# Two extra matmuls of 320 contiguous columns in a decoder-layer kernel: one a weight tile behind the first norm's sums, one a weight tile behind the prompt's value products

## The chip, the cores and the metric

The kernel runs on one core of a Trainium2 chip. Time is device microseconds of one execution. The time before is the median of three runs; a profile is of one execution of its own.

## The reference

One decoder layer is computed for 256 prompt tokens and 8 x 8 sample tokens, 320 columns in all, that share the same weights (D = 2048, feed-forward width 5632, all float32):

- xn = RMSNorm(x), and one projection W_in gives B, C, h (1024 each), q (16 heads of 64), k and v (4 heads of 64), and two gates of 2048.
- Branch A: u = C * h, a causal convolution of width 3, times B, times W_conv_out.
- Branch B: attention in a window of 128 with a relative-position bias and a sink per head, times W_attn_out. The prompt attends in two blocks of 128 queries, the sample over cached keys and values.
- m = sigmoid(gate_conv) * A + sigmoid(gate_attn) * B, then x = x + W_o(m).
- x = x + SwiGLU(RMSNorm(x)), and a final RMSNorm.

Outputs are both groups' y and the new key, value and convolution states.

## The kernel before, in words

**Products.** Activations lie transposed: a tile of 128 features by 320 tokens. Each float32 operand is split into a high part (rounded by ScalarE, `whi`, `xh`) and the rest (VectorE subtracts, `wlo`, `xl`), and a product is three matmuls: high by high, low activations by high weights, high activations by low weights. `product` (L162) makes two output blocks of 128 features at a time. It goes over weight tiles of 4 x 128 rows by 256 columns, each loaded by a DMA (`wraw`), split by ScalarE (L129) and VectorE (L130), and used by 24 matmuls (L176). The matmuls take the activations in an order of 4 x 5 x 16 columns (`turns(fives(...))`), 320 in all. In the trace a product bears the name of its output tile: q, C, H, B, gc, ga, yc, ya, wo, fg, fu; kv is `kv_product` (L372).

**Order.** The program text is the order of the work. Products follow one another: kv, q (4 pairs of blocks), then four rounds of C, H and B, then eight of gc, ga, yc, ya, then wo, then the feed-forward part. The small work between them is written as generators. After each weight tile `product` calls `tick` (L145), which takes the next step of the generator that is current, and holds that step behind the tile's last matmul:

```
def tick():
    if side_work[0] is not None:
        with after(*last.values()):
            next(side_work[0], None)
```

A `yield` in a generator therefore means one weight tile later. During the q products the generator is `kv_work`, which begins with `first_norm`; during C, H and B it is `attention`: the prompt's scores (L549, L552, tiles ps), `prompt_values` with `prompt_pv` (L611, tiles po), then `sample_attention`: scores (L716, tiles pss) and values (L779, tiles spo).

**The first norm.** In its first step `first_norm` prepares the sums of squares; a step later two matmuls against ones (`over_partitions`, L199 and L200, tile prb) sum them over the partitions, and VectorE and ScalarE make the root. Then it yields three times.

**The value products.** `prompt_values` loads the turned probabilities, one unit at a step, then calls `prompt_pv`: 80 small matmuls into four PSUM tiles, po, which ScalarE and VectorE (L642, L643) then read out. It yields once and ends, and `sample_attention` starts in the same step that the end falls in.

**The nudge.** `nudge` (L193) is a matmul whose result nobody reads. It takes the first rows of one tile as 320 contiguous columns, against 128 columns of another, and writes a tile of the pool `aux`, which has four PSUM banks taken in turn by prb, ps, po, pss, spo and the nudges. Three are there before: in `kv_product` ahead of the sixth weight tile's work (L353), in `sample_attention` a step behind the scores (L727), and in it a step behind the values (L800).

Of the kernel before, what the change touches and what calls it, by code (L numbers as in the profile page):

```python
# [17 lines left out]
T = TP + NB * TS  # L18
# [34 lines left out]
def hybrid_layer(ctx: ExitStack, tc: tile.TileContext, a: dict, o: list):  # L53
# [18 lines left out]
    def ps_aux(name):  # L72
        return aux[0].tile([P, 512], F32, tag="aux", name=name)
# [3 lines left out]
    def u(s):  # L77
        uid[0] += 1
        return f"{s}_{uid[0]}"
# [36 lines left out]
    def row_tiles(pool, names, n, lead, tags=None):  # L116

        step = n * JS + 16
        size = -(-(lead + NS * step) // JS) * JS
        tiles = [pool.tile([P, size], F32R, tag=t, name=n_) for n_, t in zip(names, tags or names)]  # L120
        return [rows_in(t, lead, step, lambda k: k * JS) for t in tiles]
# [65 lines left out]
    def two_rows(src, hi, lo):  # L187

        nc.scalar.activation(hi, fives(src), AF.Copy)
        nc.vector.tensor_sub(fives(lo), fives(src), hi.bitcast(F32))  # L190
        return hi, lo

    def nudge(rows, weights, n):  # L193
        x, w = (bass.AP(r.tensor, r.offset, [list(r.ap[0]), [1, m]]) for r, m in ((rows(0), n), (weights(0), P)))
        nc.tensor.matmul(ps_aux(u("nudge"))[:, :n], w, x, start=True, stop=True)

    def over_partitions(out, parts):
        hi, lo = parts
        nc.tensor.matmul(turns(fives(out)), ones_r, turns(hi), start=True, stop=False)  # L199
        nc.tensor.matmul(out, ones_r, lo, start=False, stop=True)  # L200
# [22 lines left out]
    def rstd_of(ss, shape, name, pool, out=None):  # L223

        v = pool.tile(shape, F32, tag=f"rs_v{shape[1]}", name=u(name))
        nc.vector.tensor_scalar(v, ss, 1.0 / D, EPS, op0=ALU.mult, op1=ALU.add)
        return inv_root(v, shape, name, pool, out)
# [26 lines left out]
    xh, xl = row_tiles(xp, ("xh_t", "xl_t"), KC, LEAD_X, ("xh", "xl"))  # L254
# [139 lines left out]
    def squares(*chunks):  # L394

        for k in chunks:
            t = tmp("t" + "abcd"[k % 4], "sq")[:, :T] if k else xacc
            nc.scalar.activation(t, hT[:, k, :], AF.Square)
            if k:
                nc.vector.tensor_add(xacc, xacc, t)  # L400
# [32 lines left out]
    def first_norm():  # L433

        squares(12, 13, 14, 15)
        nc.vector.tensor_scalar(nsink, sink_bc, -1.0, None, op0=ALU.mult)
        e_sb = pr.tile([P, 2, 2 * WIN], F32, tag="w", name="e_sb", bufs=1).rearrange("p g k -> p (g k)")[:NH, :EL]
        nc.vector.memset(e_sb, NEG)
        parts = two_rows(xacc, at_h(7), at_t[:, LEAD_A + 6 * at_row:LEAD_A + 6 * at_row + T])
        at, one_each = [_bucket(c) for c in range(WIN)], NBK // 2  # L440
        nc.gpsimd.tensor_copy(e_sb[:, WIN - 1:WIN - 1 + one_each], relT[:, :one_each])
        for b in range(one_each, NBK):
            c, n = WIN - 1 + at.index(b), at.count(b)
            nc.gpsimd.tensor_copy(e_sb[:, c:c + n], relT[:, b:b + 1].to_broadcast([NH, n]))
        yield
        prb = ps_aux("prb")
        over_partitions(prb[:, :T], parts)
        rstd_of(prb[:, :T], [P, T], "r1", spare, out=rb)
        nc.vector.tensor_scalar(rbq, rb, HD ** -0.5, None, op0=ALU.mult)
        for z in (vT, kT):  # L450
            for c in range(2):
                nc.vector.tensor_mul(z[:, c, :], z[:, c, :], rb)
        nc.vector.tensor_mul(rbsq, rb, rb)
        nc.gpsimd.dma_start(e_scr, e_sb)
        nc.gpsimd.dma_start(
            bias_s, bass.AP(e_scr.tensor, e_scr.offset + WIN - TS, [[EL, NH], [1, TS], [1, WIN + TS]])
        )
        for _ in range(3):
            yield

    yp = ExitStack()
    yy = yp.enter_context(tc.tile_pool(name="yy", bufs=1))
# [135 lines left out]
    def prompt_masked(sides, pt, side):  # L598

        late = by_head(pt[:, :, 2:4])  # L600
        for out, m in ((side, 0), (late, 1)):
            mask = sides[:, m].rearrange("p (a j) -> p a j", j=B).unsqueeze(1).to_broadcast([P, 2, 4, B])
            nc.vector.tensor_mul(out, late, mask)

    def prompt_pv(pts, side, vm):
        po, step = [ps_aux(u("po")) for _ in range(4)], 2 * JS + 16

        def add(bank, kv, cols, w, x, start, stop):
            vals = slice(kv * HD, (kv + 1) * HD)
            out = po[bank][kv % 2 * 64:kv % 2 * 64 + 64, cols]  # L610
            nc.tensor.matmul(  # L611
                out.rearrange("p (g a j) -> p g a j", g=2, j=B), w[:, vals], x, start=start, stop=stop
            )

        for bank in range(4):
            for par in range(2):
                kv = bank // 2 * 2 + par
                add(bank, kv, slice(0, 256), vn[0], by_head(pts[kv][:, bank % 2, :, 0:2]), True, False)
        for whole in (True, False):
            for j in range(2):  # L620
                cols = slice(256 + j * 128, 384 + j * 128)
                for bank in range(4):
                    rows = slice(0, P) if whole else slice(bank * B, (bank + 1) * B)
                    for kv in (2 * j, 2 * j + 1):
                        x = pts[kv][:, :, bank, 2:4] if whole else side[kv][rows, :, :, bank]
                        add(bank, kv, cols, vm[bank] if whole else vn[0][rows], x, False, not whole and j == 1)
        for bank in range(4):
            src = po[bank][:, 0:256].rearrange("p (g s j) -> p g s j", g=2, j=JS)
            dst = at_chunks(2 * bank, 2)[:, :, 0:2 * step].rearrange("p g (s j) -> p g s j", s=2)
            two_to(dst[:, :, :, 0:JS], dst[:, :, :, JS:2 * JS], src)  # L630
        for bank in range(4):
            src = po[bank][:, 256:512].rearrange("p (c j) -> p c j", j=B)
            o = (2 + bank // 2) * step + bank % 2 * B
            two_to(*(at_chunks(0, 8)[:, :, o1:o1 + B] for o1 in (o, o + JS)), src)
# [27 lines left out]
    def prompt_values(pv, scrs):  # L662
        sides = pv.tile([P, 2, WIN], F32, name="sides")
        nc.gpsimd.memset(sides, 1.0)
        nc.gpsimd.affine_select(
            out=sides[:, 0], in_=sides[:, 0], compare_op=ALU.is_ge, fill=0.0, base=-1, pattern=[[-1, WIN]],
            channel_multiplier=1,
        )
        nc.gpsimd.affine_select(
            out=sides[:, 0], in_=sides[:, 0], compare_op=ALU.is_ge, fill=0.0, base=B - 1, pattern=[[B, 4], [0, B]],  # L670
            channel_multiplier=-1,
        )
        nc.gpsimd.tensor_tensor(sides[:, 1], sides[:, 1], sides[:, 0], op=ALU.subtract)
        pts = [pv.tile([P, 2, 4, 4, B], F32, name=f"pT{kv}") for kv in range(NKV)]
        side = [pv.tile([P, 2, 2, 4, B], F32, name=f"side{kv}") for kv in range(NKV)]
        vm = [pv.tile([P, DKV], F32, name=f"vm{t}") for t in range(3)] + [vn[1]]
        mixes = ((0, 0, P, 0), (0, 0, B, 1), (1, 0, P, 0), (1, 0, 2 * B, 1), (2, 0, P, 1), (2, 3 * B, P, 0))
        for i in range(len(units) + 5):
            if i < len(units):
                kv, gp = units[i]  # L680
                nc.gpsimd.dma_start(pts[kv][:, gp].rearrange("p a n j -> p (a n j)"), scrs[i])
            if 2 <= i < 8:
                t, r0, r1, src = mixes[i - 2]
                nc.scalar.activation(vm[t][r0:r1], vn[src][r0:r1], AF.Copy)
            if i >= 5:
                kv, gp = units[i - 5]
                prompt_masked(sides, pts[kv][:, gp], side[kv][:, gp])
            yield
        prompt_pv(pts, side, vm)
        yield  # L690

    W2 = WIN + TS

# [132 lines left out]
    def kv_work():  # L826
        yield from first_norm()
        rows = []
        for t in range(3):
            rows.append(kv_turn(t))  # L830
            yield
        yield from keys_twice()
        for t in range(3):
            kv_natural(t, rows[t])
            yield
# [190 lines left out]
    def h_parts(k):  # L1026
        return parts_of(hT[:, k, :])
# [250 lines left out]
    for c in (2, 3):  # L1278
        k = E0 // P + c
        first, _ = h_parts(k)  # L1280
# [53 lines left out]
def _bucket(dist):  # L1334
    half = NBK // 2
    if dist < half:
        return dist
    return min(half + int(math.log(dist / half) / math.log(WIN / half) * (NBK - half)), NBK - 1)
# [61 lines left out]
```

## Time and profile before

| | |
|---|---|
| median of 3 runs | 1590.14 us (1590.08 to 1590.64) |
| profiled execution | 1589.86 us |
| its span, first to last instruction | 1588.1 us |
| mean granted TensorE clock | 0.999 |
| TensorE busy | 1580.0 us, 99%, 11315 matmuls |
| VectorE, ScalarE, GpSimd busy | 881.6, 651.4, 128.5 us |
| read from HBM | 257.25 MB, 168 GB/s with the writes |

A matmul's duration in the trace (301 ns for 320 columns) is longer than its slot, because matmuls overlap. What counts is the distance from one start to the next. The chain of waits merges neighbouring matmuls of a line into one row with a length and a count, and length over count is that distance.

### The profile page before, as it was taken

Reading aid. Unit: us, or ns where it says so; the run is one execution under the profiler, and the core shown is the slowest. Engines: PE = TensorE matmul, PEld = TensorE weight load, DVE = VectorE, ACT = ScalarE, POOL = GpSimd, SP = SyncE. Lnnn points to the kernel's source line nnn. Section 1 sums busy time; section 2 is a strip of 40 time slices with the busy share of each in tenths; the row PEclk is TensorE's granted clock in tenths of the full one; section 3 lists DMA queues with packets and bytes.
Section 4 is the critical chain, followed back from the end, with each engine's and each line's share of the span. In section 5 each row is a group of like instructions: output and inputs, shape, how many; then the busy total and the mean of one; then the engine's idle time right before and its main releaser. Section 6 shows DMA issues by size and latency. Waiting matters only on the chain.

```text
span 1588.1 us, 27217 instructions
## 1 busy us (share of the span) xinstructions
PE 1580.0 (99%) x11315; PEld 1566.3 (99%) x11315; DVE 881.6 (56%) x1263; ACT 651.4 (41%) x913; POOL 128.5 (8%) x228
## 2 busy tenths in 40 slices
PE   9999999999999999999999999999999999999998
PEld 9999999999999999999999999999999999999887
DVE  7888765544455445565555555553443455555556
ACT  7554444333333334344333333333333333344443
POOL 2223242000000003320000000000000000000000
PEclk9999999999999999999999999999999999999999
DMA  8666666454444544444444445455555544544653
GB/s 276 204 191 193 213 205 207 160 157 157 152 158 159 159 158 153 156 158 160 157 153 156 158 159 159 154 154 158 159 159 156 155 157 158 160 159 152 186 191 122
DMA packets 77714, 266.09 MB, mean 168 GB/s; under 512 B 9816, under 2 KB 13240, under 8 KB 77464
## 3 DMA queue, kind: packets, MB, share of 16 engines
q1 hardware_dynamic: 71880, 249.86, 49.7%
q0 software_dynamic: 5280, 13.82, 2.9%
q8 instruction: 88, 1.44, 0.4%
q10 hardware_dynamic: 432, 0.69, 0.1%
q14 instruction: 34, 0.28, 0.1%
HBM read 257.25 MB, written 9.04 MB: 168 GB/s over the span
## 4 chain that ended last, share of the span: by engine, by line
PE 99%; DVE 0%; ACT 0%; DVEq 0%; issue 0%
PE fu L176 19%; PE fg L176 19%; PE dn L1059 12%; PE wo L176 7%; PE ga L176 7%; PE gc L176 7%; PE B L176 3%; PE H L176 3%; PE C L176 3%; PE q L176 3%; PE ya L176 3%; PE yc L176 3%; PE dn L1084 3%; PE kv L372 2%; PE dn L1092 2%; PE dl L1088 1%
## 5 line engine op out<-in xcount | busy, mean ns | idle before, releaser
L130 DVE TENSOR_TENSOR wlo<-wraw,whi 128x1024 fp32r<-128x1024 f32 (+1 forms) x460 | 560.9, 1220 | 574.3 <-ACT whi L129 563.4
L129 ACT ACTIVATE whi<-wraw 128x1024 fp32r<-128x1024 f32 (+1 forms) x460 | 485.0, 1056 | 699.5 <-PE fu L176 131.5
L176 PE MATMUL fu<-hh_t,whi 128*128 128x320 f32 x704 | 205.0, 301 | 0.0
L176 PE MATMUL fu<-hl_t,whi 128*128 128x320 f32 x704 | 205.0, 301 | 0.0
L176 PE MATMUL fg<-hh_t,whi 128*128 128x320 f32 x704 | 205.0, 301 | 0.0
L176 PE MATMUL fg<-hl_t,whi 128*128 128x320 f32 x704 | 205.0, 301 | 0.0
L1059 PE MATMUL dn<-a_t,whi 128*128 128x320 f32 x896 | 162.6, 301 | 0.0
L176 PE MATMUL fg<-hh_t,wlo 128*128 128x320 f32 x704 | 158.8, 301 | 0.0
L176 PE MATMUL fu<-hh_t,wlo 128*128 128x320 f32 x704 | 158.8, 301 | 0.0
L1059 PEld LDWEIGHTS dn<-a_t,whi 128*128 128x128 f32 x896 | 137.5, 187 | 0.0
L176 PEld LDWEIGHTS fu<-hh_t,whi 128*128 128x128 f32 x704 | 131.7, 187 | 0.0
L176 PEld LDWEIGHTS fu<-hl_t,whi 128*128 128x128 f32 x704 | 131.6, 187 | 0.0
L176 PEld LDWEIGHTS fg<-hh_t,whi 128*128 128x128 f32 x704 | 131.6, 187 | 0.0
L176 PEld LDWEIGHTS fg<-hl_t,whi 128*128 128x128 f32 x704 | 131.6, 187 | 0.0
L176 PEld LDWEIGHTS fg<-hh_t,wlo 128*128 128x128 f32 x704 | 116.1, 187 | 0.0
L176 PEld LDWEIGHTS fu<-hh_t,wlo 128*128 128x128 f32 x704 | 116.1, 187 | 0.0
L1059 PE MATMUL dn<-a_t,wlo 128*128 128x320 f32 x448 | 103.9, 301 | 0.0
L1059 PEld LDWEIGHTS dn<-a_t,wlo 128*128 128x128 f32 x448 | 74.8, 187 | 0.0
L176 PE MATMUL gc<-xh_t,whi 128*128 128x320 f32 x256 | 74.5, 301 | 0.0
L176 PE MATMUL gc<-xl_t,whi 128*128 128x320 f32 x256 | 74.5, 301 | 0.0
L176 PE MATMUL ga<-xh_t,whi 128*128 128x320 f32 x256 | 74.5, 301 | 0.0
L176 PE MATMUL ga<-xl_t,whi 128*128 128x320 f32 x256 | 74.5, 301 | 0.0
(328 smaller groups left out, 2801.9 us busy)
## 6 DMA issues: line engine op xcount, KB each, us to landing
wraw<-in_w_in_dram SPq DMA_DIRECT2D x128, 512.0 KB, 3.7
wraw<-in_w_gate_dram SPq DMA_DIRECT2D x88, 512.0 KB, 3.6
wraw<-in_w_up_dram SPq DMA_DIRECT2D x88, 512.0 KB, 3.6
wraw<-in_w_down_dram SPq DMA_DIRECT2D x88, 512.0 KB, 3.6
wraw<-in_w_o_dram SPq DMA_DIRECT2D x32, 512.0 KB, 3.6
wraw<-in_w_conv_out_dram SPq DMA_DIRECT2D x16, 512.0 KB, 3.7
wraw<-in_w_attn_out_dram SPq DMA_DIRECT2D x16, 512.0 KB, 3.8
wraw<-in_w_kv_dram SPq DMA_DIRECT2D x6, 512.0 KB, 7.6
```

The source lines that it names most:

```text
L129: last["hi"] = nc.scalar.activation(hi, src, AF.Copy)
L130: last["lo"] = nc.vector.tensor_sub(lo, src, hi.bitcast(F32))
L176: last["mm"] = nc.tensor.matmul(turns(fives(ps[c][:, :T])), w[:, k, c * P:(c + 1) * P], turns(x(kc)), start=(kc == 0 and i == 0), stop=(kc ...
L372: last["mm"] = nc.tensor.matmul(turns(fives(ps[c][:, :T])), w[:, k, c * P:(c + 1) * P], turns(x(kc)), start=(kc == 0 and m == 0), stop=(kc ...
L1059: last["mm"] = nc.tensor.matmul(turns(fives(ps[c][:, :T])), parts[k][w][:, c * P:(c + 1) * P], turns(x(k)), start=k == 0 and m == 0, stop= ...
L1084: nc.tensor.matmul(turns(placed(ps[c])), parts[k][0][:, cs], turns(a_move(k)), start=k == 0, stop=False)
L1088: nc.tensor.matmul(low, a_low(k), parts[k][0], start=k == 0, stop=k == nf - 1)
L1092: last["mm"] = nc.tensor.matmul(turns(placed(ps[c])[:, :, 0:JT]), parts[k][1][:, cs], turns(a_move(k)[:, :, 0:JT]), start=False, stop=k == ...
```

## The change

Two calls of `nudge(xh, xl, T)` are added, T being 320. The first stands in `first_norm`, one step behind the step that holds the sums; the number of yields stays three. The second stands in `prompt_values` behind the yield that follows `prompt_pv`, ahead of the first step of `sample_attention`.

```diff
@@ -455,8 +455,10 @@
         nc.gpsimd.dma_start(
             bias_s, bass.AP(e_scr.tensor, e_scr.offset + WIN - TS, [[EL, NH], [1, TS], [1, WIN + TS]])
         )
-        for _ in range(3):
-            yield
+        yield
+        nudge(xh, xl, T)
+        yield
+        yield
 
     yp = ExitStack()
     yy = yp.enter_context(tc.tile_pool(name="yy", bufs=1))
@@ -688,6 +690,7 @@
             yield
         prompt_pv(pts, side, vm)
         yield
+        nudge(xh, xl, T)
 
     W2 = WIN + TS
 
```

## The prediction

> **What bounds the kernel now.** I read the page first: the span, the busy shares, the clock row and the chain that ended last.
>
> ```profile
> span 1588.1 us, 27217 instructions
> ## 1 busy us (share of the span) xinstructions
> PE 1580.0 (99%) x11315; PEld 1566.3 (99%) x11315; DVE 881.6 (56%) x1263; ACT 651.4 (41%) x913; POOL 128.5 (8%) x228
> ...
> PEclk9999999999999999999999999999999999999999
> ...
> PE 99%; DVE 0%; ACT 0%; DVEq 0%; issue 0%
> ```
>
> The chain is TensorE for 99% of the span, at a granted clock of 0.9 or more in every slice. Next I asked who waits for whom, to see whether TensorE itself is kept waiting.
>
> ```profile
> ACT whi L129 <- PE fu L176: 131.5, 76, 2.6
> ```
>
> It is the other way round: ScalarE, which splits the weights, waits for TensorE to free the weight buffers (131.5 us in 76 times at one product alone, by the columns of that row). So the weights are ahead, and the time is the number of matmuls times the pace at which TensorE takes them. An added matmul adds its own slot; nothing hides it. The only thing that could pay for it is a better pace of the matmuls behind it. The third view is therefore the chain of waits in order of time (start us, us, what, count), which gives the pace as length over count. Near the first site:
>
> ```profile
> 15.53 0.15 PE nudge L195
> 15.68 16.82 PE kv L372 x120
> 32.50 6.72 PE q L176 x48
> 39.22 0.14 PE prb L199
> 39.36 0.15 PE prb L200
> 39.51 47.04 PE q L176 x336
> 86.55 3.36 PE C L176 x24
> 89.91 0.23 PE ps L549 x2
> ```
>
> And near the second:
>
> ```profile
> 196.42 4.25 PE po L611 x80
> 200.67 3.61 PE H L176 x24
> 204.28 10.24 PE B L176 x72
> 214.52 1.13 PE pss L716 x64
> 215.65 3.61 PE B L176 x24
> 219.25 0.15 PE nudge L195
> 219.40 13.44 PE C L176 x96
> ...
> 251.46 3.58 PE B L176 x24
> 255.04 0.15 PE nudge L195
> 255.19 6.74 PE B L176 x48
> ```
>
> The reader is to divide. 47.04/336, 3.36/24 and 13.44/96 are all 140.0 ns a matmul. One row is different: 10.24/72 is 142.2 ns. It stands between the prompt's value products (po) and the sample's scores (pss), and its tile is of the same shape. So TensorE has two paces for the same instruction here, a steady 140.0 and a loose 142.2, and the loose one lasts until something shifts the stream: the matmul named nudge at 219.25 is followed by 140.0 again. The rows of single matmuls show how the loose pace looks and how it ends (start us, us, ...):
>
> ```profile
> 218.38 0.30 PE L176 MATMUL B<-xl_t,whi 128*128 128x320 f32 x1
> 218.53 0.73 PE L176 MATMUL B<-xh_t,wlo 128*128 128x320 f32 x4
> 219.09 0.31 PE L195 MATMUL nudge<-xh_t,xl_t 128*128 128x320 f32 x1
> 219.24 0.30 PE L176 MATMUL C<-xh_t,whi 128*128 128x320 f32 x1
> 219.38 0.30 PE L176 MATMUL C<-xl_t,whi 128*128 128x320 f32 x1
> ```
>
> From 218.38 to the nudge at 219.09 there are five starts in 0.71 us, 142 ns each; the nudge takes a slot of 0.15, and the next start is 0.14 behind.
>
> **The change, first matmul.** It is issued one weight tile, 24 matmuls, behind the two matmuls of the norm's sums (prb), so after 39.51 + 24 x 0.140 = 42.87 us. In this trace that place is already at 140.0 (47.04/336 covers it), so there is no loose pace to mend. Its price is from the two nudges that stand in a steady stretch. The one at 15.53 takes 0.15, and the 120 matmuls behind it take 16.82 where 120 x 0.140 is 16.80. The one at 255.04 takes 0.15, and its 48 take 6.74 where 48 x 0.140 is 6.72. So 0.15 + 0.02 = +0.17 us. Bounds: at least the slot of a plain matmul, 0.14; a gain behind it is excluded unless a pace under 140.0 exists, and no row of this shape shows one. The upper bound is a nudge that leaves the loose pace behind (a rival below).
>
> By the Trainium skill, page "TensorE: Matmul & The Clock Gate", section "Back-to-back issue gap", a warm matmul's slot is N/2.4 + 2.5 ns, an estimate of 135.8 ns for 320 columns. The rows here say 140.0 for the products and 150 for a nudge, and I go by the rows. By the page's figure the two nudges would cost 0.27 us together instead of 0.32.
>
> **The change, second matmul.** The value products end, 24 matmuls of H follow (200.67, x24), and at the next weight tile the nudge is issued, at about 204.3, ahead of the 72 B matmuls. Its slot is 0.15, as at 219.25, where the stream came in at the loose pace too and nothing was lost behind it. Its gain is the loose pace of those 72: 10.24 - 72 x 0.140 = 10.24 - 10.08 = 0.16 us. Then come the sample's scores and 24 more matmuls of B, 3.61 us in the row at 215.65, which holds the restart behind the scores. The like row behind the sample's values, 251.46, takes 3.58 with a steady stream. So if the scores too now leave a steady pace, 0.03 more is gained here. If they do, the old nudge at 219.25 comes out of a steady stream and costs 0.17, not 0.15. The two cancel within 0.01, and I take nothing for either.
>
> Does this nudge wait? It writes a bank of the four that the value products, scores and nudges share in turn, and so takes over the bank of the first of four po tiles. That one must have been emptied.
>
> ```profile
> 201.09 2.74 DVE L643 TENSOR_TENSOR at_t<-po,at_t 128x256 fp32r<-128x256 f32 x8 [2.88 <-ACT at_t L642]
> 203.75 0.41 DVE L885 TENSOR_TENSOR ue<-H,csb 128x256 f32<-128x256 f32 x1
> ```
>
> The eight subtractions that empty all four end at 203.83 (201.09 + 2.74), before 204.2, and the first bank's last reader is the fifth of them. So the wait is nil; if VectorE were late, TensorE would stand still with the B product behind it, one for one. The sample's scores, 10 us later, find their four banks one place further in the turn, all free. The first nudge takes the bank after prb's, unused at that time. No DMA is issued, no queue is passed, and no step moves: the three bare stops of the first norm's work and the one behind the value products stay as many as they were. The operands are the two halves of x, in place since the first product.
>
> **The sum.** +0.17 + 0.15 - 0.16 = +0.16 us. The profiled execution took 1589.86 (span 1588.1, and 1.76 outside it); it would take 1590.02. It stands 0.28 under the median of the runs, 1590.14; the same step on the median gives 1590.30. A measurement of this kernel tells about 0.2% (3.2 us) from no change, so this is no change.
>
> **Rivals.** *A. Slower: the last nudge lands on the loose pace.* The stream's phase at 204 is changed, and the later events (scores, nudge, values, nudge) start from another phase. If the nudge at 255.04 then leaves 142.2, that lasts to the next foreign matmuls, the second norm's sums:
>
> ```profile
> 705.45 0.14 PE pss L199
> 705.59 0.15 PE pss L200
> 705.74 13.44 PE fu L176 x96
> ```
>
> That is (705.45 - 255.19)/0.140 = 3,216 matmuls by 2.2 ns: +7.1 us, 1597.4, if it mends there. It decides from 3.2/0.0022 = 1,450 matmuls, some 200 us, of loose pace. For it speaks that two of the foreign groups, the value products and the sample's scores, do leave the loose pace. Against it, all three nudges in the trace (15.53, 219.25, 255.04) are followed by 140.0, whichever pace they came from, and so are both norms' sums (39.51 and 705.74). 4 in 100.
>
> *B. The first nudge itself loosens the pace.* Then it lasts to the prompt's first scores (ps, at 89.91). 336 - 24 = 312 matmuls of q and 24 of C by 2.2 ns are +0.74 us: 1591.0. If the scores do not mend it, it goes on to the value products at 196: about 1,000 matmuls, +2.3 us, 1592.6, still under the bound. Against it, again, the three nudges; for it, that the place is steady and can only be disturbed. 6 in 100.
>
> *C. The second nudge does not mend the pace*, so the change is two bare matmuls: +0.17 + 0.15 = +0.32, 1590.46. For it: the mending is shown by one nudge (219.25) only, and between two products rather than behind H and ahead of B; but its neighbours are the same instructions. 12 in 100. [...]
>
> *D. The first nudge changes the phase that the value products start from, and these then leave a steady pace by themselves.* Then H and B gain some 0.05 and 0.16, and both nudges cost 0.17: +0.13, 1590.27. 8 in 100. A gain over 0.2% has no place to come from: the loose matmuls that I find in the trace, 24 + 72 + 24 by 2.2 ns, hold 0.26 us together. 1 in 100 for what I do not see.
>
> **How the numbers follow.** The forecast has 69 in 100, D 8, C 12, B 6, A 4, and 1 for a gain unseen. Within 0.2%: 69 + 8 + 12 + 6 = 95; slower 4; faster 1. The time is the forecast's, 1590.3. The range: the forecast, C and D lie between 1590.2 and 1590.5; the runs of before lie between 1590.08 and 1590.64 and the profiled one at 1589.86, so a median can stand some 0.3 lower or higher. Below, 1590.27 less 0.4 is 1589.9; above, B's first bound 1591.0 is taken in.
>
> **What the profile after would show.** In the chain of waits: a nudge of 0.15 at about 42.9 with q matmuls behind it at 140.0, some 0.02 over in the first eight; a nudge at about 204.6 (0.17 later, as all that follows the first), and the B row of 72 in 10.08 to 10.10, not 10.24; from the scores on, the same rows as before, 0.15 to 0.2 later. The q row at 142.2 would show B; the B row at 10.24, C; the H row behind the value products at a steady 0.14, D; a row of gc, ga or wo above 140.0, A. The prediction is wrong if any long row, above all those between 255 and 705 us, leaves 140.0.

## The result and the profile after

The changed kernel: 1602.41 us, median of 22 executions (1589.99 to 1603.14). The kernel before: 1590.24 (1589.63 to 1603.14, 22 executions, which include the three of the time before). The ratio over all executions, not that of the two medians, is 1.0064, 95% interval [1.0051, 1.0077]. The prediction was 1590.3 and no change. But both kernels have the same two levels, near 1590 and near 1602, with hardly anything between: of the kernel before 19 of 22 executions lie at the lower one, of the changed kernel 2 of 22. What was measured is a difference in how often an execution ends at which level, and the runs below ask what the levels are and whether the change moves the share. Two executions far from both levels, one of 3,294.88 us and one of 2,007.49 us, are in none of the counts below.

The profiled execution of the changed kernel took 1602.35 us, so it shows the upper level. Its page:

```profile
span 1600.6 us, 27222 instructions
PE 1592.4 (99%) x11317; PEld 1578.1 (99%) x11317; DVE 882.8 (55%) x1263; ACT 651.7 (41%) x913; POOL 128.2 (8%) x228
```

Still TensorE for 99%, two matmuls more, 12.5 us more span; the granted clock is 0.999 as before. Now the chain of waits in order of time (start us, us, what, count), at the two sites:

```profile
39.65 3.38 PE q L176 x24
43.03 0.15 PE nudge L195
43.17 43.70 PE q L176 x312
...
200.99 3.62 PE H L176 x24
204.61 0.14 PE nudge L195
204.75 10.09 PE B L176 x72
214.84 1.13 PE pss L719 x64
215.97 3.57 PE B L176 x24
219.54 0.15 PE nudge L195
...
249.95 1.81 PE spo L782 x117
251.77 3.61 PE B L176 x24
255.37 0.15 PE nudge L195
```

The first nudge takes 0.15 and the 312 matmuls behind it 0.02 over 43.68; the second takes 0.14, and the B row of 72 is 10.09 in place of 10.24. That is the forecast, term by term. The nudge at 255.37 starts 0.33 later than its like at 255.04 in the kernel before, 0.14 of which was there ahead of the first site (prb at 39.36 against 39.22). That part is not the change's: ahead of the first norm's sums the stream is loose in this profile and steady in the one before (6.72 for the same 48 matmuls), the change comes only behind them, and the kernel before has a loose stream there too in a later profile.

```profile
32.43 6.94 PE q L176 x48
39.36 0.14 PE prb L199
```

The rest of the 12.5 us comes 450 us later, at the second norm's sums:

```profile
692.32 13.45 PE fg L176 x96
705.77 0.14 PE pss L199
705.91 0.15 PE pss L200
706.06 13.65 PE fu L176 x96
719.71 13.65 PE fg L176 x96
...
1074.70 191.15 PE dn L1062 x1344
```

In the first profile of the kernel before, the same view has

```profile
719.18 13.44 PE fg L176 x96
...
1068.62 188.16 PE dn L1059 x1344
```

13.65/96 is 142.2 ns, and 191.15/1344 is 142.2 as well: from 706 us on the stream has the loose pace, and nothing mends it to the end of the feed-forward products. 43 rows of fg and fu by 0.213 us and 2.99 us for dn are 12.2 us; with the 0.33 from before, 12.5. A difference between the two profiles stands already ahead of the sums, at the steady pace itself. The tile view of gc (count, duration ns min/median/max, first and last start) has in the changed kernel

```profile
L176 PE MATMUL gc<-xh_t,whi x128: 302/302/302, 262.1 to 395.6; 128*128 128x320 f32 x128
```

and in the kernel before

```profile
L176 PE MATMUL gc<-xh_t,whi x128: 301/301/301, 261.8 to 395.3; 128*128 128x320 f32 x128
```

Both at 140.0 ns from start to start, but with matmuls of 302 ns in the one and 301 in the other. This nanosecond went with what the sums left in every later profile with a steady stretch there.

### The profile page after: what moved, and what is told of

The parts are those of the page before. It is cut to its first block, busy times and chain, and to the rows that moved or that the text cites. A ratio compares the mean times of both kernels' runs of the same rounds, so it can differ in the third digit from the quotient of the medians.

```text
span 1600.6 us, 27222 instructions
## 1 busy us (share of the span) xinstructions
PE 1592.4 (99%) x11317; PEld 1578.1 (99%) x11317; DVE 882.8 (55%) x1263; ACT 651.7 (41%) x913; POOL 128.2 (8%) x228
## 4 chain that ended last, share of the span: by engine, by line
PE 99%; DMA 1%; ACT 0%; DVE 0%; SPq 0%; DVEq 0%; issue 0%; ACTq 0%
PE fu L176 19%; PE fg L176 19%; PE dn L1062 12%; PE wo L176 7%; PE ga L176 7%; PE gc L176 7%; PE B L176 3%; PE H L176 3%; PE q L176 3%; PE C L176 3%; PE ya L176 3%; PE yc L176 3%; PE dn L1087 3%; PE dn L1095 2%; PE kv L372 1%; PE dl L1091 1%
```

## Experiments

### The parts of the change, an ordinary matmul, and a nudge behind the second norm's sums

The first theory was that the change sets the phase of the stream from 204 us on, and with it what the second norm's sums leave. The rival was a shift by two instructions or 0.3 us. Four kernels, on one chip, beside 33 executions of the kernel before.

First matmul alone (the changed kernel without the second):

```diff
         prompt_pv(pts, side, vm)
         yield
-        nudge(xh, xl, T)
```

> Only the first of the two matmuls is added. Phase theory (the 12 us are the loose pace of 142.2 ns behind the second norm's sums, and whether those sums tip the stream there depends on the phase that the last nudge at 255 us left): the value products still leave the loose pace, so all from 204 to 705 us goes as in the kernel before; most executions at 1590.3 (0.17 over before), q row at 140.0, the B row of 72 at 10.24, the rows behind 705 at 13.44. Rival (two more instructions or 0.3 us of delay move the second norm's sums against something else in the program): one matmul is half of it, so executions anywhere between the kernels, some at 1602.

Second matmul alone (the first norm's three bare yields again):

> Only the second matmul is added. Phase theory: B runs at 140.0 from 204 us, the sample's scores and values now start from a steady stream, and the nudge at 255 us starts from another phase than in the kernel before, as in the changed kernel; so most executions at 1602.3, with rows of 13.65 behind 705 us and 13.44 ahead of it. Rival (instruction count or delay): as with the first alone, half the change; the two should look alike.

Both as ordinary matmuls, at the two sites (one is shown):

```diff
+    def plain(xk):
+        w = ones_r
+        nc.tensor.matmul(turns(fives(ps_aux(u("plain"))[:, :T])), w, turns(xk), start=True, stop=True)
...
-        nudge(xh, xl, T)
+        plain(xh(0))
```

> Both matmuls are added at their sites, but as ordinary ones: the first rows of x in the products' own column order against the block of ones, result unread. Phase theory: an ordinary matmul does not shift the stream, so everything else goes as in the kernel before: 1590.14 + 2 x 0.14 = 1590.4 in most executions, B still at 142.2. Rival (count or delay): two more instruction pairs and 0.28 us as in the changed kernel, so most executions at 1602.

A nudge more, behind the sums:

```diff
+    def iter_nudge():
+        nudge(hh, hl, T)
+        yield
...
                 rstd_of(pss[:, :T], [P, T], "r2", hp, out=rb2)
+                side_work[0] = iter_nudge()
```

> The changed kernel with a third added nudge, one weight tile behind the second norm's sums, at about 709 us. If the 12 us are the loose pace behind those sums and nothing else: 24 matmuls of fu at 142.2 and then 140.0 again, 1590.14 + 0.3 + 0.15 + 0.05 = 1590.6 in nearly all executions. If the second level has another cause (the whole program late, a slower clock, a DMA), it stays at 1602.

Executions at the lower level: first alone 2 of 12, second alone 0 of 12, ordinary matmuls 0 of 12, the nudge behind the sums 10 of 10 (1590.09 to 1591.08). But the kernel before itself had only 8 of 33 here, where the first comparison had 19 of 22. So the three counts near zero say little: on this chip the kernel before was mostly at the upper level too.

The last kernel does say something. Its chain behind the sums:

```profile
706.09 3.41 PE fu L176 x24
709.50 0.15 PE nudge L195
709.64 10.08 PE fu L176 x72
719.73 13.44 PE fg L176 x96
```

3.41/24 is 142.1, and behind the nudge 10.08/72 and 13.44/96 are 140.0. The sums left the loose pace, one matmul ended it, and no execution stayed at 1602. The upper level is the loose pace behind the second norm's sums.

The ordinary matmuls disproved my view that only a shifted column order matters. The chain of that kernel:

```profile
42.71 0.14 PE plain L199
42.85 17.21 PE q L176 x121
...
205.00 0.15 PE plain L199
205.14 10.11 PE B L176 x72
```

At 42.71 an ordinary matmul in a steady stream leaves 142.2 (17.21/121); at 205.00 one in a loose stream leaves 140 (10.11/72, with some 0.03 of settling). So a foreign matmul of either kind can move the stream from the one pace to the other, and an ordinary one did so in both directions.

### The same kernels again, without the last nudge, and with the sums in the products' column order

The kernel before, unchanged:

> The kernel before, unchanged, profiled again, because its executions were at 1590 in 8 and at 1602 in 25 of the runs beside the first experiments. If the two levels are the pace behind the second norm's sums, a profile at the upper level shows rows of 13.65 behind 705 us and 13.44 ahead of it. By the theory of phases its nudge at 219 then leaves matmuls of 301 ns where the first profile has 302, the sample's values leave 142.2, and the nudge at 255 leaves 302. By the rival (a chance at the sums themselves, whatever came before) the stretches ahead of 705 us look as in the first profile.

Its profile fell at the upper level (1602.02 us). Chain and tile view:

```profile
251.45 3.61 PE B L176 x24
255.05 0.15 PE nudge L195
...
705.44 0.14 PE pss L199
705.59 0.15 PE pss L200
705.74 13.65 PE fu L176 x96
```

```profile
L176 PE MATMUL gc<-xh_t,whi x128: 302/302/302, 261.8 to 395.3; 128*128 128x320 f32 x128
```

So the kernel before, to the instruction, takes the course that the changed kernel's profile shows: 3.61 behind the sample's values (3.58 at the lower level), 302 ns between 255 and 705 us, 13.65 behind the sums. Neither added matmul is needed for it. Two of its 12 executions were at the lower level.

The changed kernel, unchanged:

> The changed kernel, unchanged, beside the kernel before on the same chip. If the second matmul fixes the phases from 204 us on, nearly all executions are at 1602, more than of the kernel before, whatever the chip's share of the latter. If chip and session alone set the share, both have the same share.

3 of 12 at the lower level, beside 6 of 35 of the kernel before. The two shares do not differ.

The changed kernel without the old nudge behind the sample's values:

```diff
         two_to(*parts, flipped)
-        nudge(xh, xl, T)
         yield
```

> The changed kernel without the old nudge behind the sample's values. The sample's values leave the loose pace (3.61 for 24 matmuls at 252 us), and nothing mends it until the second norm's sums. Phase theory: those sums come out of the loose pace, as the first norm's sums do in the changed kernel's profile, and leave a steady one: about 3,240 matmuls by 2.22 ns, 7.2 us less the nudge, so 1590.3 + 7.0 = 1597.3 in all executions where the values leave the loose pace. Rival (the sums tip the stream, from wherever it comes): the loose pace both ahead of and behind them, 1602.4 + 7 = 1609.4.

9 of 12 at 1609.05 to 1609.64, 3 at 1590.1 to 1590.7. The rival's number came, not mine:

```profile
251.82 10.44 PE B L176 x72
262.26 13.65 PE gc L176 x96
...
699.17 13.65 PE fg L176 x96
...
713.11 13.65 PE fu L176 x96
```

The second norm's sums did not mend a loose stream here; they left it loose. This is no rule for all such sums: the first norm's came out of a loose stream in 9 of the 19 profiles and left a steady one in 8 of them (140.5 ns a matmul or less behind them, against 142.2 or more ahead). The old nudge is worth 7 us in these executions. The three at 1590 were not profiled; their time is that of values that left a steady pace.

The changed kernel with the sums in the products' order (`same` is set for the second norm's sums alone):

```diff
         nc.tensor.matmul(turns(fives(out)), ones_r, turns(hi), start=True, stop=False)
+        if same:
+            nc.tensor.matmul(turns(fives(out)), ones_r, turns(fives(lo)), start=False, stop=True)
+            return
         nc.tensor.matmul(out, ones_r, lo, start=False, stop=True)
```

> The changed kernel with the second of the two matmuls of the second norm's sums in the products' column order, 4 x 5 x 16, in place of 320 contiguous columns; the same values. If the contiguous columns are what shifts the stream there, both matmuls pass at 140 and the pace stays steady behind them: 1590.5 in all executions. If the foreign weights, the new accumulator or the reading of it tip the stream, it stays at 1602.4.

2 of 11 at the lower level, and in the profile 13.66 for the 96 fu matmuls behind the sums, with 302 ns ahead of them. So the stream is tipped there without the contiguous columns too.

### The nudge behind the sums without the change, one far ahead of them, and an ordinary matmul as mender

On one chip, beside 35 executions of the kernel before, of which 7 were at the lower level.

The kernel before with the nudge behind the sums (the edit shown above):

> The kernel before with one nudge a weight tile behind the second norm's sums and neither of the two matmuls of the change. If the upper level is the loose pace behind those sums and a nudge always mends it, all executions are at 1590.14 + 0.15 + 0.05 = 1590.35, with or without the change's matmuls; about 0.3 under the changed kernel with the same nudge (1590.69). If the second matmul of the change is needed for the mending, some executions stay at 1602.

12 of 12 at the lower level, median 1590.45; ratio to the kernel before 0.9949 [0.9925, 0.9973]. With the 10 of 10 above, 22 of 22 executions with a nudge behind the sums are there.

The changed kernel with a nudge in the first gate product:

```diff
         nc.gpsimd.dma_start(ncv, g18)
         yield
+        nudge(xh, xl, T)
```

> The changed kernel with a further nudge at about 265 us, in the first gate product, far ahead of the second norm's sums. Phase theory: at the upper level the stream there has matmuls of 302 ns; a nudge out of it leaves the other steady kind (301), and the sums then leave a steady pace: 1590.3 + 0.17 = 1590.5 in all executions. Rival (an execution is at one level or the other whatever is done ahead of the sums): about 1 in 5 executions at 1590.5, the rest at 1602.6.

1 of 12. My expectation failed: a further nudge there did not bring the executions down to the lower level. The profile fell on the one execution at the lower level (301 ns before and behind that nudge), so what it does to a stream of 302 ns is not seen.

The changed kernel, unchanged, once more:

> The changed kernel unchanged, beside the kernel before on one more chip or session. If the change moves the share of executions at the upper level, it has more of them there than the kernel before (20 of 22 against 3 of 22 in the first comparison). If the chip or the session sets the share, both have the same (9 of 12 against 29 of 35 in the second).

1 of 12, beside 7 of 35.

The changed kernel with an ordinary matmul behind the sums (the edit against the nudge there):

```diff
-        nudge(hh, hl, T)
+        nc.tensor.matmul(turns(fives(ps_aux(u("plain"))[:, :T])), ones_r, turns(hh(0)), start=True, stop=True)
```

> The changed kernel with an ordinary matmul (products' column order, against the block of ones) in place of the nudge behind the second norm's sums. If 320 contiguous columns are needed to bring the steady pace back, the rows behind 709 us stay at 142.2: 1602.4 at the upper level. If any foreign matmul does it out of the loose pace, as the ordinary one at 204.8 us did, the upper level comes down to 1590.6; executions that reach 709 us with a steady pace may be tipped by it and end at 1602.

11 of 12 at the lower level, one at 1602.63. The mending does not need contiguous columns:

```profile
706.40 3.41 PE fu L176 x24
709.81 0.14 PE plain L198
709.96 10.09 PE fu L176 x72
```

The one at 1602.63 was not profiled. It may be an execution that came steady and was tipped, as the expectation allowed.

### What follows the sample's values

The changed kernel, unchanged, a fourth time:

> The changed kernel unchanged, beside the kernel before, once more. If the change moves the share of executions at the upper level: more of them than of the kernel before, by far. If the share is the chip's or the session's: the same in both, as in the two later comparisons (21 of 24 against 57 of 70, by the runs at 1602).

The 21 of 24 in that text is 20 of 24 by the runs. 1 of 11, beside 2 of 24 of the kernel before. Over the three later comparisons together the changed kernel has 5 of 35 at the lower level and the kernel before 15 of 94. Its profile, at the upper level, adds a case:

```profile
252.04 0.30 PE L176 MATMUL B<-xl_t,whi 128*128 128x320 f32 x1
...
253.03 0.35 PE L176 MATMUL B<-xh_t,wlo 128*128 128x320 f32 x1
253.22 0.30 PE L176 MATMUL B<-xh_t,whi 128*128 128x320 f32 x1
...
254.76 0.72 PE L176 MATMUL B<-xh_t,wlo 128*128 128x320 f32 x4
```

The sample's values left the loose pace: the seven distances up to 253.03 average 142.3 ns by the starts in nanoseconds. The ninth matmul, the first on the low part of this weight tile, then takes a slot of 0.19, and behind it the 11 distances up to 254.76 average 140. So the old nudge came out of a steady stream here, and yet the tile view of gc reads

```profile
L176 PE MATMUL gc<-xh_t,whi x97: 301/302/303, 274.8 to 395.8; 128*128 128x320 f32 x97
```

that is, 302 by the median, and the sums left 142.2. What the nudge came out of, loose or steady, does not decide alone; the kind of the stream that reaches the sums goes with the level.

The old nudge behind the values as an ordinary matmul:

```diff
         two_to(*parts, flipped)
-        nudge(xh, xl, T)
+        nc.tensor.matmul(turns(fives(ps_aux(u("plain"))[:, :T])), ones_r, turns(xh(0)), start=True, stop=True)
```

> The changed kernel with an ordinary matmul (products' column order, block of ones) in place of the old nudge behind the sample's values. If the kind of the stream between 255 and 705 us decides the level: a profile at 1590 shows 301 ns there and one at 1602 shows 302, as in all profiles so far, and the share of the levels may change, since another matmul lands the stream. If the level is decided elsewhere: the share stays at about 1 in 5 at 1590, and a profile may show 301 at 1602. If the ordinary matmul does not mend: 1609.

5 of 12 at the lower level, 6 at 1602, and one at 1597.22. That one was not profiled; its time is that of rival A (1597.4), a loose pace up to the second norm's sums that these then mend. The profile (1602.64) has 302 ns and 13.65 again. More executions at the lower level than beside it, but still both.

The old nudge moved directly behind the values:

```diff
                     add(at, kv, ptn[rows, at, kv * B:(kv + 1) * B], vn[2][rows], False, b == half - 1)
+        nudge(xh, xl, T)
         yield
...
         two_to(*parts, flipped)
-        nudge(xh, xl, T)
         yield
```

> The changed kernel with the old nudge moved from one weight tile behind the sample's values to directly behind them. If the landing of the stream behind the values is what differs between executions: the nudge now always follows the same small matmuls, so nearly all executions go one way, all at 1590.2 or all at 1602.4. If the difference comes from earlier (another phase from the start of the execution): the share stays at about 1 in 5 at the lower level.

5 of 5 at the lower level (1589.88 to 1590.40). The chain:

```profile
250.12 1.82 PE spo L782 x117
251.93 0.34 PE nudge L195
252.28 10.10 PE B L176 x72
...
705.89 0.14 PE pss L199
706.03 0.14 PE pss L200
706.18 13.45 PE fu L176 x96
```

The nudge's row is 0.34 because it now holds the restart behind the small matmuls, which was in the row of 24 before (3.58 to 3.61 against 3.36). Behind it the stream is steady, with 301 ns, and the sums leave 140.1. Five executions being few, it was run again, and the same move was made in the kernel before:

> The changed kernel with its last nudge directly behind the sample's values, again, for the number of executions. If the place decides: all at 1590.3. If five of five was luck at a share of 1 in 5: mostly 1602.

> The kernel before, with neither matmul of the change, and its last nudge moved from one weight tile behind the sample's values to directly behind them. If that place alone decides: all executions at 1590.1, 0.05 to 0.1 under the lower level of the kernel before (24 matmuls off the loose pace), rows at 13.44 to the end, matmuls of 301 ns from 252 us on. If the steady B product of the change is needed, so that the scores and values start from one phase: both levels again, about 1 in 5 at 1590.

10 of 10 for the changed kernel with the move (median 1590.28) and 9 of 9 for the kernel before with it (median 1590.28, 1589.83 to 1590.73), beside 2 of 17 of the kernel before, unmoved. Ratio to it, for both: 0.9935 [0.9915, 0.9956]. The 0.05 to 0.1 us under the lower level that I expected does not show in these times. So 24 of 24 executions with the nudge in that place are at the lower level, on two chips where the kernel before is nearly always at the upper. The move costs no instruction. It and the nudge behind the sums each beat the kernel before where that is mostly at the upper level; on an occasion like the first comparison, 19 of 22 at the lower level, there was little to gain. The move is the cheaper by one matmul.

## Why the prediction was wrong, point by point

**The bound was right, and the sum by its rows.** TensorE's order sets the time. +0.17, +0.15 and -0.16 came as 0.15 + 0.02, 0.14 and -0.15. The times cannot confirm the +0.16. At the lower level the changed kernel's 7 executions in four comparisons average 1590.45 and the kernel before's 44 average 1590.29, a difference of 0.17 with a standard error of 0.16. At the upper level 50 and 122 executions average 1602.44 and 1602.43. On one chip, with the last nudge moved and all executions at the lower level, the kernel with the change averages 1590.36 and the one without it 1590.26, a difference of 0.10 with a standard error of 0.11.

**Two things that the sum has no term for.** The prediction saw no loose pace to mend at the first site. In 2 of the 14 profiles with an added matmul there the first norm's sums left one (3.41 for the 24 matmuls at 39.70 us in the fourth run of the changed kernel), and the nudge ended it. And TensorE stood still in two profiles, ahead of the ninth matmul of B behind the sample's values: 0.34 us in the kernel with a nudge behind the sums, and 0.66 us in the second run of the changed kernel:

```profile
253.54 0.42 PE L176 MATMUL B<-xh_t,wlo 128*128 128x320 f32 x1 [0.66 <-DVE oT L798]
```

The trace puts both down to VectorE. In the changed kernel's first profile no such wait appeared. Whether the change brings it is not shown.

**The step that failed** is in rival A: "Against it, all three nudges in the trace (15.53, 219.25, 255.04) are followed by 140.0, whichever pace they came from, and so are both norms' sums (39.51 and 705.74)." For the nudges this held: in every profile here the stream behind the nudges at 219 and 255 us is steady. For the sums it was one execution taken for a rule. The first norm's leave the loose pace in 2 of the 19 profiles, and those at 705 leave 142.2 in 12 of them, 11 times out of a steady stream. I put the danger at the nudge of 255 and let the sums mend it; in fact the sums are where the pace is lost, and behind them nothing stands to mend it for 5,472 matmuls, 12.2 us, against the 3,216 and 7.1 us that I priced. A loose stretch from 255 us to the sums exists as well: it is the kernel without the last nudge, where it adds 7 us and the sums left the stream loose.

**The second failure** lies under it: the chances were worked out as if one execution stood for the kernel. The three runs of before, 1590.08 to 1590.64, and the profile, 1589.86, were all of the lower level, and I took that for the spread. The question was not whether the change costs 0.16 us but how often an execution falls on the upper level. The profile could have raised it: two paces for one instruction, landings that differ, and a stretch of nearly 780 us behind 705 with no event to end a bad one.

**Did the change make the kernel slower?** In the first comparison, by the counts, yes: 20 of 22 at the upper level against 3 of 22. In the three later comparisons, no: 30 of 35 against 79 of 94. What set the kernel before so often at the lower level in the first comparison, and not the changed one, stays open; so does whether executions of one occasion are independent of each other. That the later executions of the kernel before take the same course as the changed kernel's shows that the upper level is not the change's own.

**What decides the level, as far as shown.** The kind of the stream between 255 and 705 us goes with it in all 18 profiles where that stretch is steady: 7 with 301 ns, and the sums leave 140; 11 with 302 ns, and they leave 142.2. The first norm's sums agree: 9 times they come out of 301 ns and leave 140, once out of 302 and leave 142.2. That is a sign that goes with it, not a mechanism.

The kind can be traced one step back. In 15 profiles a nudge or an ordinary matmul stands 24 matmuls behind the sample's values. In the 4 of them at 301 ns, the values left the steady pace: behind the restart stand at most three slots of up to 150 ns, then 140 (the row of 24 reads 3.57 or 3.58). In the 11 at 302 ns they left the loose one (3.61 in eight, 3.63 in the case with the slot of 0.19, and two with the waits told above). So these executions part on the first few matmuls behind the values. That the place of the last nudge fixes the level is shown by 24 of 24. Why the stream lands in two ways behind the values is open: the starts inside the values agree within 3 ns in 18 of the 19 profiles, at either level. The stream can also turn loose with no foreign matmul: it is loose ahead of the first norm's sums in 9 of the 19 profiles and steady in the other 10, with the kernel before on both sides.

The Trainium skill, page "TensorE: Matmul & The Clock Gate", section "Back-to-back issue gap", gives N/2.4 + 2.5 ns as the gap of an isolated warm matmul (135.8 ns for 320 columns, as an estimate by it), and has other spacings for a stream of weight loads and matmuls. The prediction applied that gap to a stream. The runs show two spacings in such a stream, 140.0 and 142.2, at one granted clock of 0.999.

## What to carry to other kernels

Where a kernel is one dense stream of like matmuls, look at the distance from start to start to a tenth of a nanosecond, in every long row: 2.2 ns over 5,472 matmuls is 0.8% of this kernel. After each foreign group of matmuls ask which pace it left and what stands behind it; try a cheap foreign matmul behind the last group ahead of a long stretch, or directly behind the group that lands badly, and time it often, for a matmul put into a steady stream left the loose pace once here (17.21 for 121). And before a change of tenths of a microsecond is judged, time the kernel before often enough, and on more than one chip, to see whether it has one level or two.

## What the runs showed of the hardware

- One shape of matmul (128 x 128 by 320 columns) runs at a steady 140.0 or a loose 142.2 ns from start to start, at the same granted clock, for hundreds of microseconds. A foreign matmul can move it from one to the other: out of the loose pace a nudge left a steady one in every profile.
- The steady pace has two kinds, 301 and 302 ns by the matmuls' durations. They cost the same until the next norm's sums, and differ in what these left: 140 behind 301, 142.2 behind 302, in 28 of 28 cases.
- Executions of one kernel differ in this, and the share differs by occasion, for a reason that stays open: at the lower level the kernel before had 19 of 22, 8 of 33, 6 of 35, 7 of 35, 2 of 24 and 2 of 17.
- Behind the small matmuls of the sample's values, a nudge at once (0.34 us) gave the lower level in 24 of 24 executions (301 ns in the three profiles); one 24 matmuls later gave both levels.
